# Values kept per head pair in DRAM, and transposes that take every second to fourth column

## The chip, the cores and the metric

The kernel runs on one core of a Trainium2 chip. The metric is the device time of one execution in microseconds; the time before is the median of three runs. Engines are named as the profile names them: PE (TensorE; PEld is its weight load), DVE (VectorE), ACT (ScalarE), POOL (GpSimd), SP (the engine that issues nearly all transfers).

## The reference, cut to what matters

An encoder layer over two sequences, a prompt of 256 tokens (a grid of 4 rows by 64 columns) and a sample of 2048 tokens (32 rows by 64 columns), model width 1024. A projection gives q, k, v and a gate for a neighbourhood attention with 8 heads of 64, and two more parts for a Fourier mixing branch. Both branches are normalised, gated, joined and projected back.

```python
proj = rms_norm(x, g_pre) @ w_in
q, k, v, z_a, u_f, z_f = split(proj)
# attention: a query at (r, c) sees the keys of 8 rows by 16 columns around it
logits = einsum(q, k_window) * scale + bias
p = softmax(logits)
y_a = einsum(p, v_window)
y_f = fft2(u_f).real @ w_f + b_f
out = x + rms_norm(concat(rms_norm(y_a)*silu(z_a), rms_norm(y_f)*silu(z_f)) @ w_out, g_post)
```

## The kernel before, in words

Everything is float32; the large products are made of three products of rounded parts each (`mm3`). The kernel first runs the input projection, stage by stage, and stores q, k, v, gates and the Fourier input in DRAM tensors (up to about 548 us of the profile). Then come the Fourier branch's transforms (to about 613 us), attention (to about 850 us), and the last output projection. The order of the work on every engine is written out by hand: `vu`, the loop over `i` and `j` of the projection with its hooks, and in attention one loop over `k` in which each engine's instructions are issued in a fixed order. SP works through one queue of transfers in program order and waits in it.

**v on its way to attention.** `put_rows` stores a finished tile of v of the sample (128 tokens by 512 features, all 8 heads) in the DRAM tensor `vN`, indexed by column half, row, column and feature (L361, 16 tiles of v and 16 of u, u into `uN`). Six copies from DRAM to DRAM (`v_copy`, L368, one per step `i` from 9 to 14 of the projection) gather from `vN` the four column blocks of 23, 31, 31 and 24 columns that attention reads, into `vD[0]` to `vD[3]`, each with 32 rows. The prompt's v is stored apart, in `vP`.

**Attention in groups.** There are 4 head pairs (128 features) and 9 groups for each: group 0 is the prompt, groups 1 to 8 are four row windows of the sample (11, 15, 15 or 12 key rows, `NR`, from row `K0`) times two column halves. Each group has two column blocks, so its keys number rows times columns, 160 to 465 for each block. `scores` makes the logits (L1225), `bias_max` and `exps` the exponentials, `soft` (L1259, POOL) divides by the sums; all stand in the tile `w`, 128 queries by keys, for two heads.

The product with v needs the keys on the partitions. So a block of n keys is cut into m pieces of at most 128 keys, with m from 2 to 4. `prep_v` loads the pieces of v, with z partitions (a multiple of 8) to a piece, and lists them in `g["ch"]` as (first column, number of keys, place in the tile `v`). `transp` (L1577) transposes each piece of `w` on PE into PSUM: the piece is loaded as weights, the identity of 128 columns streams through. ACT copies the first head's pieces to SBUF (L1579), DVE the second's (L1581). `pv` (L1593) multiplies each piece with its piece of v. Before the change, piece x is the consecutive keys from z*x on:

```python
z = min(-(-n // m) + 7 & ~7, 128)
ch = [(z * x, min(z, n - z * x), j + x) for x in range(m)]
```

For n = 465 that gives pieces of 120, 120, 120 and 105 keys. Over a head pair there are 55 pieces, each for two heads: 440 transposes and 880 products in the kernel. The load of v takes 512 B per key and partition, since one key's 128 features of the head pair stand in a row of 512 floats.

In the loop over `k`, the group k gets its scores while the group k - 1 is transposed and multiplied with v; the load of v for group k + 1 (`prep_v`) is issued at the end of step k. The tile `v` has three buffers (`VB`).

Of the kernel before, what the change touches and what calls it, by code (L numbers as in the profile page):

```python
# [10 lines left out]
F32 = mybir.dt.float32  # L11
# [19 lines left out]
K0 = (0, 4, 12, 20)  # L31
KW = (23, 31, 31, 24)
# [142 lines left out]
def build(tc, A, O):  # L175
    nc = tc.nc
# [3 lines left out]
    dr = es.enter_context(tc.tile_pool(name="dr", bufs=1, space=DRAM))  # L180
# [1 line left out]
    qD = dr.tile([4, 128, T], F32, name="qD")  # L182
    kD = dr.tile([4, 128, T], F32, name="kD")

    vD = [dr.tile([32, w, 512], F32, name="vD%d" % i) for i, w in enumerate(KW)]
    vP = dr.tile([2, 4, 40, 512], F32, name="vP")
    zD = dr.tile([2, 512, T], F32, name="zD")
    ZD = dr.tile([128, 16, 512], F32, name="ZD")
    uD = dr.tile([TP, 512], F32, name="uD")

    vN, uN = [dr.tile([2, 32, 32, 512], F32, name=n) for n in ("vN", "uN")]
    sD = dr.tile([5, 128, 4, 512], F32, name="sD")
    xD = dr.tile([7, 128, 4, 512], F32, name="xD")
    ivD = dr.tile([18, 128], F32, name="ivD")
# [5 lines left out]
    ident = cst.tile([128, 128], F32, name="ident")  # L200
# [24 lines left out]
    def mmt(n):  # L225
        x = mmc[0] % 5 > 2
        mmc[0] += 1
        return ps.tile([128, n], F32, tag="t" if x else "a", name="mm", bufs=2 if x else 3)
# [115 lines left out]
    def vu_out(m, c):  # L344
        s, b = PL[c]
        o = st.tile([128, 512], F32, tag="f", name=m + "o", bufs=3)
        x = row_tile(c)
        nc.scalar.activation(o, acc.pop((m, c)), AF.Copy, scale=invt[:, x:x + 1])
        if s is not None:
            put_rows(m, 0, b, s, o)  # L350
        elif m == "u":
            nc.sync.dma_start(uD[c * 128:c * 128 + 128, :], o)
        else:
            for r in range(4):
                nc.sync.dma_start(vP[c, r, 8 * c:8 * c + 32], o[32 * r:32 * r + 32])
                x = 24 * (1 - c)
                nc.sync.dma_start(vP[1 - c, r, 32 * c:32 * c + 8], o[32 * r + x:32 * r + x + 8])

    def put_rows(m, sg, b, s, o):
        r = 16 * sg + 4 * s  # L360
        nc.sync.dma_start((vN if m == "v" else uN)[b, r:r + 4].rearrange("r c e -> (r c) e"), o)  # L361


    VC = ((0, 0, 0, 23, 0), (1, 0, 8, 24, 0), (1, 1, 0, 7, 24), (2, 0, 24, 8, 0), (2, 1, 0, 23, 8), (3, 1, 8, 24, 0))

    def v_copy(i):
        x, b, c0, n, d0 = VC[i]
        nc.sync.dma_start(vD[x][:, d0:d0 + n], vN[b][:, c0:c0 + n])  # L368


    uu_ = {}
# [125 lines left out]
    def vu(sg, S, hooks):  # L497
# [7 lines left out]
        for i, (j, s) in enumerate(seq):  # L505
            for x in loads.get(i, ()):
                op_load(x)
            if i in splits:
                op_split(splits[i])
            for f in hooks.get(i, ()):  # L510
                f()
            p = mmt(512)
            h, l = op_[j]
            th, tl = bnew[sg, j]
            for k in range(4):
                mm3(nc, p, th[:, k, 128 * s:128 * s + 128], tl[:, k, 128 * s:128 * s + 128], h[k // 2][:, k % 2],
                    l[k // 2][:, k % 2], k == 0, k == 3)
            T2 = lambda o, a: nc.vector.tensor_tensor(out=o, in0=a, in1=p, op=ALU.add)
            if j == 0:
                uc[s] = et("uc")  # L520
                nc.scalar.copy(uc[s], p)
            elif j == 2:
                T2(uc[s], uc[s])
            elif j == 3:
                u4[s] = et("u4")
                T2(u4[s], uc[s])
            else:
                o = st.tile([128, 512], F32, tag="f", name="vuo", bufs=3)
                T2(o, (u4 if j in (4, 6) else uc)[s])
                if j == 4:  # L530
                    T2(uc[s], uc[s])
                put_rows("v" if j in (1, 6) else "u", sg, int(j in (4, 6)), s, o)
# [104 lines left out]
    for kp in range(4):  # L637
        ks = slice(2 * kp, 2 * kp + 2)
        v = part(RV[kp // 2], kp)
# [131 lines left out]
    for b in range(16):  # L771
# [13 lines left out]
        if 2 <= b < 8:  # L785
            x, y = divmod(b, 2)
# [9 lines left out]
        p = mmt(512)[:, :TP]  # L796
# [3 lines left out]
        o = st.tile([128, 256], F32, tag="f", name="f", bufs=3)  # L800
        if kind % 2:
            i, d = p, o
        else:
            i = p.rearrange("p (b r c) -> p b r c", b=2, c=32)
            d = o.rearrange("p (r b c) -> p b r c", b=2, c=32)
# [47 lines left out]
    for i in range(16):  # L853
        sg, pr = divmod(i, 8)
# [14 lines left out]
        o = [st.tile([128, 1024], F32, tag="f", name="f", bufs=3) for x in range(2)]  # L869
# [31 lines left out]
        for j in range(7):  # L901
            for f, d in ((u_load, 0), (u_split, 4), (u_stage1, 6)):
                x = 7 * pr + j - 7 - d
# [33 lines left out]
            if sg == 0:  # L937
                x, y = divmod(7 * (pr - 1) + j, 14)
# [27 lines left out]
            if 9 <= i < 15 and j == 2:  # L966
                v_copy(i - 9)
            p = mmt(512)
# [34 lines left out]
    ptb = [ps.tile([128, 512], F32, tag="t", name="ptb", bufs=2) for i in range(2)]  # L1003
# [179 lines left out]
    def prep_v(g):  # L1183
        cs = slice(g["pr"] * 128, g["pr"] * 128 + 128)
        g["v"] = jl.tile([128, 7, 128], F32, tag="v", name="v", bufs=VB)
        g["ch"], j = [], 0
        for b, (c0, w) in enumerate(g["t"]):
            n = g["nr"] * w
            src = (vP[b] if g["R"] is None else vD[2 * g["hc"] + b][K0[g["R"]]:]).rearrange("r c e -> (r c) e")
            m = -(-n // 128)  # L1190
            z = min(-(-n // m) + 7 & ~7, 128)
            f = m if src.shape[0] >= m * z else n // z
            nc.sync.dma_start(g["v"][:z, j:j + f], src[:z * f, cs].rearrange("(j p) e -> p j e", p=z))
            if f < m:
                nc.sync.dma_start(g["v"][:n - z * f, j + f], src[z * f:n, cs])
            ch = [(z * x, min(z, n - z * x), j + x) for x in range(m)]
            g["ch"].append(ch)
            j += len(ch)
        g["za"] = jl.tile([128, 256], F32, tag="za", name="za", bufs=VB)
        nc.sync.dma_start(g["za"], zD[1, cs, g["ts"]])  # L1200

# [69 lines left out]
    for g in G[:2]:  # L1271
        prep(g)
        prep_v(g)
# [11 lines left out]
    for t, (g, x) in enumerate(zip(G, (0, 640))):  # L1285
        g["w"] = []
        for c0, w in g["t"]:
            n = 2 * g["nr"] * w
# [281 lines left out]

    def transp(g, b):
        ch = g["ch"][b]
        n, z = len(ch) * 128, ch[0][1]
        o = jp.tile([128, 2, 512], F32, tag="pt", name="pt", bufs=PB)
        for h in range(2):
            for j, (c0, nk, v) in enumerate(ch):
                nc.tensor.transpose(ptb[h][:nk, j * 128:j * 128 + 128], g["w"][b][:, h, c0:c0 + nk], ident)  # L1577
            if h == 0:
                nc.scalar.copy(o[:z, h, :n], ptb[h][:z, :n])  # L1579
            else:  # L1580
                V.tensor_copy(o[:z, h, :n], ptb[h][:z, :n])  # L1581
        g["pt"] = g.get("pt", []) + [o]
# [109 lines left out]
    def part(P, name, n):  # L1692
        return [sm.tile([128, n, 128], F32R, tag="y%s%d" % (x, n) if n < 4 else "y" + x, name="y" + x,
                        bufs=3 if n == 4 else 1) for x in "hl"]
# [103 lines left out]
    prep(G[4])  # L1798
    f_mm(0)
    transp(G[0], 0)  # L1800
    f_norm(range(2))
    transp(G[0], 1)
    soft(G[1], 1)
    run_later()
# [4 lines left out]
    pv(G[0])  # L1809
    ys_load(ftiles[2])  # L1810
    prep_v(G[2])
    split_q(G[3])
    prep(G[5])
    ones32 = sm.tile([128, 32], F32, name="ones32", bufs=1)
    nc.vector.memset(ones32, 1.0)
    for k in range(2, len(G) + 1):
        pr, i = divmod(k, 9)
        g, f = G[k] if k < len(G) else None, G[k - 1] if k else None
# [14 lines left out]
        if k == 28:  # L1833
            for c, x in enumerate(("kh", "kl")):
                w = kp.tile([128, T], F32R, tag=x, name="wk")
                WO[c] = [w[:, 56 + D * y:56 + D * y + D] for y in range(2)]
        if k in WK:
            c, y = WK[k]
# [3 lines left out]
        x = k // 2 + 1  # L1842
# [11 lines left out]
        if not g:  # L1854
            a_mm(atiles[0], 0, range(6))
        transp(f, 0)
        if g:
            exps(g, 0, 1)
# [57 lines left out]
        if k + 1 < len(G):  # L1916
            prep_v(G[k + 1])
# [123 lines left out]
```

## Time and profile before

| | us |
|---|---|
| median of three runs | 959.93 (957.2 to 960.42) |
| profiled execution | 958.19 |
| its span, first to last instruction | 956.4 |
| PE busy | 944.8 (99% of the span) |
| PE weight loads busy | 784.3 (82%) |
| DVE / ACT / POOL busy | 732.0 / 505.8 / 453.3 |

The granted clock of PE is 0.997 over the span. The DMA queue that carries nearly everything moves 270.68 MB in 140,352 packets and takes 82.9% of the sixteen DMA engines' time. A line such as "L1577 PE MATMUL ptb<-ident,w 128*120 128x128 f32 x204 | 33.1, 278" names the source line, the engine, the operation, the output and inputs, the weights' rows and columns (128*120), what streams through (128x128), the count, and then the busy time in us and the mean duration of one in ns. Durations of matmuls overlap, so what one costs is read from the spacing of their starts.

### The profile page before, as it was taken

To read this page: it belongs to the slowest core of one execution; us is meant where nothing else is said; L and a number is where in the kernel's file an instruction comes from. 1 tells how busy PE (TensorE), PEld (TensorE's weight loads), DVE (VectorE), ACT (ScalarE), POOL (GpSimd) and SP (SyncE) were. 2 spreads that over 40 slices of the span, in tenths; PEclk is the share of its full clock that TensorE was granted. 3 is DMA by queue.
4 is the path that set the end of the run, shared out by engine and by line. 5 is a ranking of instruction groups with operands and counts; after the bars stand their busy time and mean duration, and the time that the engine had idled before them with its cause. 6 is when DMAs were issued, how large, how long until landed. Compare 5 with 4: busy or idle time off the path is not lost.

```text
span 956.4 us, 16730 instructions
## 1 busy us (share of the span) xinstructions
PE 944.8 (99%) x5595; PEld 784.3 (82%) x5595; DVE 732.0 (77%) x1347; ACT 505.8 (53%) x1088; POOL 453.3 (47%) x426
## 2 busy tenths in 40 slices
PE   9999999999999999999999999999999999999996
PEld 7889988888888888888888879788787888788885
DVE  6758987788876765698887369777888878759876
ACT  6835676433334532233344267677876777654443
POOL 4100002464751302575566045567899798624444
PEclk9999999999999999999999999999999999999998
DMA  9899697557848894499889996698998999889995
GB/s 356 298 385 336 243 339 270 189 201 270 299 188 323 314 341 144 175 352 361 300 289 338 338 341 246 215 276 281 309 253 253 290 280 312 239 296 327 305 317 197
DMA packets 140790, 272.17 MB, mean 285 GB/s; under 512 B 12854, under 2 KB 80664, under 8 KB 137440
## 3 DMA queue, kind: packets, MB, share of 16 engines
q1 hardware_dynamic: 140352, 270.68, 82.9%
q8 instruction: 45, 0.74, 0.3%
q10 hardware_dynamic: 288, 0.40, 0.1%
q14 instruction: 41, 0.34, 0.1%
q0 software_dynamic: 64, 0.02, 0.0%
HBM read 181.37 MB, written 96.81 MB: 291 GB/s over the span
## 4 chain that ended last, share of the span: by engine, by line
PE 89%; DMA 4%; DVE 2%; POOL 2%; ACT 1%; issue 1%; SPq 0%; DVEq 0%; POOLq 0%; ACTq 0%
PE mm L166 18%; PE mm L164 18%; PE mm L165 18%; PE po L1504 10%; PE ptb L1577 5%; PE pv L1593 5%; PE s L1225 4%; DMA yr<-yD 2%; PE px L1689 2%; PE pz L1689 2%; DMA yo<-xt 1%; PE py L164 1%; PE py L165 1%; PE py L166 1%; PE ptb L1043 1%
## 5 line engine op out<-in xcount | busy, mean ns | idle before, releaser
L164 PE MATMUL mm<-xh,wa 128*128 128x512 f32 x448 | 174.4, 389 | 0.0
L166 PE MATMUL mm<-xh,wa 128*128 128x512 f32 x448 | 174.3, 389 | 0.0
L165 PE MATMUL mm<-xl,wa 128*128 128x512 f32 x448 | 174.3, 389 | 0.0
L545 POOL TENSOR_TENSOR ws<-wr 128x512 f32<-128x512 f32 x16 | 22.6, 1415 | 219.3 <-DMA wr<-wz 215.6
L1259 POOL TENSOR_SCALAR w<-w,m 128x465 f32<-128x465 f32 (+9 forms) x136 | 89.3, 670 | 32.7 <-DVE m L1256 13.5
L165 PEld LDWEIGHTS mm<-xl,wa 128*128 128x128 f32 x448 | 84.1, 188 | 17.5
L164 PEld LDWEIGHTS mm<-xh,wa 128*128 128x128 f32 x448 | 84.1, 188 | 17.5
L166 PEld LDWEIGHTS mm<-xh,wa 128*128 128x128 f32 x448 | 84.1, 188 | 17.4
L560 DVE TENSOR_TENSOR wa<-wr,wa 128x512 fp32r<-128x512 f32 x60 | 75.4, 1264 | 21.9 <-ACT wa L559 21.6
L1504 PE MATMUL po<-wk,yh 128*128 128x512 f32 x280 | 87.1, 392 | 0.9 <-ACT yh L1490 0.9
L1252 ACT ACTIVATE w<-w,m 128x465 f32<-128x465 f32 (+9 forms) x136 | 78.4, 579 | 14.3 <-DVE m L1247 13.6
L1968 POOL TENSOR_TENSOR xt<-of,xt 128x512 f32<-128x512 f32 x34 | 43.2, 1293 | 54.6 <-issue 33.0
L1247 DVE CUSTOM_DVE_ANT_1 w<-s,tb 128x465 f32<-128x465 f32 (+8 forms) x124 | 61.4, 529 | 8.9 <-PE s L1225 8.0
L598 POOL TENSOR_TENSOR mt<-mt,rmask 128x880 f32<-128x880 f32 (+2 forms) x24 | 50.3, 2111 | 32.6 <-DVE mt L594 26.2
L164 PE MATMUL mm<-vh,xh 128*128 128x512 f32 x168 | 65.4, 389 | 0.0
L165 PE MATMUL mm<-vl,xh 128*128 128x512 f32 x168 | 65.4, 389 | 0.0
L166 PE MATMUL mm<-vh,xl 128*128 128x512 f32 x168 | 65.4, 389 | 0.0
L1504 PEld LDWEIGHTS po<-wk,yh 128*128 128x128 f32 x280 | 52.1, 188 | 12.2 <-ACT yh L1490 1.3
L891 DVE TENSOR_TENSOR f<-u,mm 128x512 f32<-128x512 f32 x64 | 43.4, 679 | 23.3 <-PE mm L166 18.5
L1577 PE MATMUL ptb<-ident,w 128*120 128x128 f32 (+8 forms) x422 | 59.0, 277 | 1.4 <-ACT pt L1579 1.2
L559 ACT CAST wa<-wr 128x512 fp32r<-128x512 f32 x60 | 36.5, 618 | 43.5 <-PE mm L166 20.4
L1577 PEld LDWEIGHTS ptb<-ident,w 128*120 128x120 f32 (+8 forms) x422 | 47.1, 140 | 14.5 <-issue 4.6
(332 smaller groups left out, 2469.3 us busy)
## 6 DMA issues: line engine op xcount, KB each, us to landing
wr<-wz SPq DMA_DIRECT2D x48, 512.0 KB
vl<-sD SPq DMA_DIRECT2D x20, 512.0 KB
xm<-xm SPq DMA_DIRECT2D x9, 1024.0 KB
oD<-ofs SPq DMA_DIRECT2D x18, 512.0 KB
of<-oD SPq DMA_DIRECT2D x18, 512.0 KB
xt<-xn SPq DMA_DIRECT2D x18, 512.0 KB
yo<-xt SPq DMA_DIRECT2D x35, 256.0 KB
yr<-yD SPq DMA_DIRECT2D x34, 256.0 KB
```

Source lines behind the costliest of these rows:

```text
L164: nc.tensor.matmul(out, lh, rh, start=first, stop=False)
L165: nc.tensor.matmul(out, lh, rl, start=False, stop=False)
L166: nc.tensor.matmul(out, ll, rh, start=False, stop=last)
L560: nc.vector.tensor_tensor(out=o[:, 1], in0=src, in1=o[:, 0].bitcast(F32), op=ALU.subtract)
L598: nc.gpsimd.tensor_tensor(out=o, in0=i, in1=rmask[:, m0:m0 + n].unsqueeze(2).to_broadcast([128, n, 80]), op=ALU.add)
L891: nc.vector.tensor_tensor(out=dst(f, b), in0=src(uu[u]), in1=src(p), op=op)
L1247: nc.vector.tensor_tensor_reduce(out=rows(g["w"][b][:, h, :n], w), in0=rows(g["s"][2 * b + h][:, :nr * sw(w)], sw(w))[:, :, :w], in1=tv, s ...
L1252: nc.scalar.activation(w, w, AF.Exp, bias=m[:, h:h + 1], scale=-1.0, accum_out=m[:, 2 + h:3 + h])
L1259: nc.gpsimd.tensor_scalar(w, w, m[:, 4 + h:5 + h], 1.0, ALU.mult, ALU.mult)
L1504: nc.tensor.matmul(p, (d["l"] if x == 2 else d["h"])[:, c], w(n, int(x == 1), c), start=j == 0, stop=j == 11)
L1577: nc.tensor.transpose(ptb[h][:nk, j * 128:j * 128 + 128], g["w"][b][:, h, c0:c0 + nk], ident)
L1593: nc.tensor.matmul(p[hs, b], g["v"][:nk, v, hs], g["pt"][b][:nk, h, j * 128:j * 128 + 128], start=j == 0, stop=j == len(ch) - 1)
```

## The change

v of the sample is stored per head pair: `vN` and `vD` get the head pair as an outer dimension and rows of 128 floats, so that consecutive keys of one head pair follow each other in memory. A store of v writes four pieces of 512 B for each partition. `prep_v` puts m consecutive keys on one partition, so one packet of the load has 2 to 4 keys; piece x of a block is now the keys x, x + m, x + 2m and so on. `transp` therefore takes every m-th column of `w`, and takes an even number of them where the tile is wide enough (one column more than needed, whose result is not used). The loads still cover a multiple of 8 partitions, where the tensor's end allows it, else a multiple of 16 and a second load for the rest. The number of keys in a piece becomes nearly equal: for n = 465, 118, 116, 116 and 116 columns are transposed.

```diff
-    vD = [dr.tile([32, w, 512], F32, name="vD%d" % i) for i, w in enumerate(KW)]
+    vD = [dr.tile([4, 32, w, 128], F32, name="vD%d" % i) for i, w in enumerate(KW)]
...
-    vN, uN = [dr.tile([2, 32, 32, 512], F32, name=n) for n in ("vN", "uN")]
+    vN = dr.tile([2, 4, 32, 32, 128], F32, name="vN")
+    uN = dr.tile([2, 32, 32, 512], F32, name="uN")
...
     def put_rows(m, sg, b, s, o):
         r = 16 * sg + 4 * s
-        nc.sync.dma_start((vN if m == "v" else uN)[b, r:r + 4].rearrange("r c e -> (r c) e"), o)
+        if m == "v":
+            nc.sync.dma_start(vN[b, :, r:r + 4].rearrange("h r c e -> (r c) h e"), o.rearrange("p (h e) -> p h e", h=4))
+        else:
+            nc.sync.dma_start(uN[b, r:r + 4].rearrange("r c e -> (r c) e"), o)
...
     def v_copy(i):
         x, b, c0, n, d0 = VC[i]
-        nc.sync.dma_start(vD[x][:, d0:d0 + n], vN[b][:, c0:c0 + n])
+        nc.sync.dma_start(vD[x][:, :, d0:d0 + n], vN[b][:, :, c0:c0 + n])
...
             n = g["nr"] * w
-            src = (vP[b] if g["R"] is None else vD[2 * g["hc"] + b][K0[g["R"]]:]).rearrange("r c e -> (r c) e")
             m = -(-n // 128)
-            z = min(-(-n // m) + 7 & ~7, 128)
-            f = m if src.shape[0] >= m * z else n // z
-            nc.sync.dma_start(g["v"][:z, j:j + f], src[:z * f, cs].rearrange("(j p) e -> p j e", p=z))
-            if f < m:
-                nc.sync.dma_start(g["v"][:n - z * f, j + f], src[z * f:n, cs])
-            ch = [(z * x, min(z, n - z * x), j + x) for x in range(m)]
-            g["ch"].append(ch)
-            j += len(ch)
+            z = -(-n // m) + 1 & ~1
+            if g["R"] is None:
+                src = vP[b].rearrange("r c e -> (r c) e")
+                nc.sync.dma_start(g["v"][:z, j:j + m], src[:, cs].rearrange("(p j) e -> p j e", j=m))
+            else:
+                src = vD[2 * g["hc"] + b][g["pr"]].rearrange("r c e -> (r c) e")
+                k0 = K0[g["R"]] * w
+                y = z + 7 & ~7
+                y = y if k0 + y * m <= src.shape[0] else z & ~15
+                for p0, p1 in ((0, y), (y, z)):
+                    if p0 < p1:
+                        nc.sync.dma_start(g["v"][p0:p1, j:j + m],
+                                          src[k0 + p0 * m:k0 + p1 * m].rearrange("(p j) e -> p j e", j=m))
+            g["ch"].append([(x, -(-(n - x) // m), j + x) for x in range(m)])
+            j += m
...
     def transp(g, b):
         ch = g["ch"][b]
-        n, z = len(ch) * 128, ch[0][1]
+        m, z = len(ch), ch[0][1] + 1 & ~1
+        n = 128 * m
...
             for j, (c0, nk, v) in enumerate(ch):
-                nc.tensor.transpose(ptb[h][:nk, j * 128:j * 128 + 128], g["w"][b][:, h, c0:c0 + nk], ident)
+                y = nk + 1 & ~1
+                y = y if c0 + m * y - m < g["w"][b].shape[2] else nk
+                nc.tensor.transpose(ptb[h][:y, j * 128:j * 128 + 128], g["w"][b][:, h, c0:c0 + m * y - m + 1:m], ident)
```

## The prediction

> **What bounds the kernel now.** I read the page's parts 1 and 2 first, then the time by stretches, then what TensorE waited for, then the groups of the lines that the diff touches.
>
> ```profile
> span 956.4 us, 16730 instructions
> PE 944.8 (99%) x5595; PEld 784.3 (82%) x5595; DVE 732.0 (77%) x1347; ACT 505.8 (53%) x1088; POOL 453.3 (47%) x426
> DMA  9899697557848894499889996698998999889995
> DMA packets 140790, 272.17 MB, mean 285 GB/s; under 512 B 12854, under 2 KB 80664, under 8 KB 137440
> PE 89%; DMA 4%; DVE 2%; POOL 2%; ACT 1%; issue 1%; SPq 0%; DVEq 0%; POOLq 0%; ACTq 0%
> ...
> 613.00:740.00 127.00, 125.80 (x1115) 100.84 (x1115) 100.71 (x301) 97.47 (x277) 103.00 (x124) 1.00 0.92 271
> 740.00:850.00 110.00, 109.66 (x993) 88.89 (x991) 84.77 (x252) 76.11 (x218) 80.84 (x112) 1.00 0.96 281
> 850.00:948.00 98.00, 97.14 (x444) 79.81 (x439) 78.35 (x174) 44.31 (x125) 42.23 (x34) 1.00 0.90 300
> 948.00:956.40 8.40, 0.42 (x4) 0.27 (x3) 5.18 (x14) 1.52 (x6) 2.99 (x3) 0.71 0.44 158
> ```
>
> The first number after a stretch's length is PE's busy time. Attention's transposes and products run from 613 to 850 us: PE lacks 127.00 - 125.80 = 1.20 us there and then 110.00 - 109.66 = 0.34 us; in the last projection it lacks 0.86 us. The DMA engines are busy too (0.92, 0.96), but a busy DMA engine only costs time where PE waits for it. So the next view is what PE waited for, the whole list:
>
> ```profile
> PE ptb L1577 <- ACT pt L1579: 1.2, 2, 0.7
> PE idle L237 <- POOL onesq L233: 1.0, 1, 1.0
> PE po L1504 <- ACT yh L1490: 0.9, 1, 0.9
> PE ptb L1577 <- POOL ysq L1614: 0.2, 1, 0.2
> PE mm L170 <- DVE xl L296: 0.2, 1, 0.2
> ```
>
> The columns are waiter and releaser, microseconds in total, times, longest wait. No DMA stands in it. The kernel is a queue of TensorE work; a change in it counts at full price, and a change elsewhere counts for at most the 2.4 us that PE lacks between 613 and 948 us (1.20 + 0.34 + 0.86).
>
> **The change part by part.**
>
> *1. The loads of v (the loop in prep_v).* 84 issues before (L1193 with 72, L1195 with 12), 84 after: one per window and column block, and a second one for the three narrow blocks of the last window row, in each of 4 head pairs. By the nine sizes of issue (from the view of DMA issues, the first and the last in the fence below) they move 12,456 KB, in rows of 128 floats (512 B): 24,900 packets. After, one packet holds 2, 3 or 4 keys; counting the partitions that the new code loads (1,992 per head pair) gives about 8,000. Writing v by head pair turns 16 stores of 128 packets into 16 of 512: +6,100. The six DRAM copies go from 32 runs to 128 each: +600. In all 140,790 becomes about 130,500, with the same bytes. The gain is hidden completely: each load is issued about two groups before its products, into three buffers, and no row of PE's waits names it. So I set it to 0, with 2.4 us as the most that it could give back.
>
> ```profile
> v<-vD SPq DMA_DIRECT2D x24, 180.0 KB
> ...
> v<-vD SPq DMA_DIRECT2D x4, 42.0 KB
> ...
> L1193 SPq DMA_DIRECT2D v<-vD x64: 311/452/2680, 562.5 to 830.4; - x64
> L361 SPq DMA_DIRECT2D vN<-vuo x12: 319/320/867, 128.4 to 385.8; - x12
> L368 SPq DMA_DIRECT2D vD<-vN x6: 473/474/564, 412.8 to 516.5; - x6
> SPq L361 <- DVE vuo L518: 60.7, 22, 7.8
> ```
>
> *2. The stores and copies.* The three numbers after an L line's count are the shortest, median and longest issue in ns. A store whose partitions each hold four pieces should issue like the loads of several pieces (452 ns) and no longer like one piece (320 ns): 16 x 0.13 = 2.1 us of SP's time. Queued behind it on SP are the stores of u, the weight loads and the reloads of u. SP's queue stood 60.7 us at this very line waiting for VectorE's results, so it has that time. DVE, ACT and POOL gain no instruction. Cost 0; if the cover went, 2.1 us spread over 350 us. The copies keep their 473 ns issues and their bytes; what they could cost otherwise is a rival below.
>
> *3. The copies out of PSUM, and the products with v.* The counts do not change: 440 transposes by the code (4 head pairs, 2 heads, 55 pieces), as many PSUM-to-SBUF copies over the same 256 to 512 columns, 880 products. A copy covers fewer partitions (114 to 124 in place of 120 or 128), a product contracts fewer rows, which costs the same at 128, 120 and 105 rows (283, 277 and 272 ns). Cost 0.
>
> ```profile
> L1593 PE MATMUL pv<-pt,v 120*64 120x128 f32 x416 | 30.7, 277 | 0.0
> L1593 PE MATMUL pv<-pt,v 105*64 105x128 f32 x96 | 9.5, 272 | 0.0
> L1593 PE MATMUL pv<-pt,v 128*64 128x128 f32 x80 | 6.9, 283 | 0.0
> ```
>
> *4. The transposes: where the price is open.* A transpose loads a piece of w as weights and streams the 128 columns of the identity. The piece was consecutive columns; now it is every 2nd (48 transposes), 3rd (264) or 4th (128) column, an even number of them, 80 to 128.
>
> ```profile
> L1577 PEld LDWEIGHTS ptb<-ident,w 128*120 128x120 f32 x204 | 23.3, 137 | 8.8 <-issue 3.8 <-POOL w L1259 1.8 <-POOL kl L1141 0.9
> L1577 PEld LDWEIGHTS ptb<-ident,w 128*105 128x105 f32 x48 | 8.2, 171 | 0.0
> L1577 PEld LDWEIGHTS ptb<-ident,w 128*128 128x128 f32 x38 | 4.8, 140 | 1.3
> L1577 PEld LDWEIGHTS ptb<-ident,w 128*80 128x80 f32 x24 | 2.5, 118 | 1.1 <-issue 0.4 <-POOL yr L1481 0.2
> ...
> 638.85 1.04 PE L1577 MATMUL ptb<-ident,w 128*120 128x128 f32 x8
> 639.64 0.48 PE L1504 MATMUL po<-wo,yh 128*128 128x512 f32 x1
> ...
> 646.80 0.82 PE L1577 MATMUL ptb<-ident,w 128*120 128x128 f32 x6
> 647.37 0.71 PE L1504 MATMUL po<-wo,yh 128*128 128x512 f32 x2
> ...
> L1551 PEld LDWEIGHTS ptb<-sqs,ones x32: 106/108/110, 619.3 to 657.9; 128*32 128x32 f32 x32
> L1034 PEld LDWEIGHTS pup<-f,up x4: 135/137/160, 567.4 to 567.7; 128*32 128x32 f32 x4
> L1034 PEld LDWEIGHTS ptb<-f,up x16: 186/192/192, 565.4 to 567.1; 128*128 128x128 f32 x16
> ```
>
> First the spacing. Six transposes of 120 columns start at 646.80, and the next product at 647.37; eight transposes, of which the program makes two of 105 columns, take 638.85 to 639.64. The two more cost 0.79 - 0.57 = 0.22 us, so 110 ns each, odd pieces or not. The identity's stream sets this; the load for the next transpose runs beside it and is free as long as it streams in under about 109 ns.
>
> Then the loads. Even pieces: 118 ns for 80 columns, 140 for 128, which is 22 / 48 = 0.46 ns per column over a fixed 81 ns. The odd piece: (171 - 81) / 105 = 0.86 ns per column, nearly twice that, and yet free, because 105 x 0.86 = 90 ns is under 109. So evening out the odd pieces gains 0.
>
> Now the step. The trace has one load with a step, the 32 columns that the code takes eight apart for up (pup): 137 ns against 108 ns for 32 consecutive ones. With the same 81 ns that is 1.75 against 0.84 ns per column, a factor of 2.1. It is an ordinary load; the changed transposes step by 2 to 4. Ends for the price: below, 0 (a load that is free cannot become freer); above, 1.75 ns per column for every stepped piece, so 203 ns in place of 109 at 116 columns. Summed over the 440 pieces by width (48 of 114, 144 of 116, 32 of 118, 48 of 120, 48 of 124, the rest narrower or 126 and 128) that end is +37.6 us. Between them: if the pairwise fetch of even pieces survives and only slows by the same factor, 2.1 x 0.46 = 0.96 ns per column; 116 columns then take 111 ns (2 over), 120 take 115 (6 over), 124 take 119 (10 over), in sum +1.5 us. I take half of that, +0.8 us: the row of odd pieces shows that a halved rate is hidden, and the steps are shorter than the eight that was measured. What is hidden here is hidden by the identity's stream; beyond 109 ns every ns is paid 440 times on the bounding engine.
>
> **Sum.** 0 + 0 + 0 + 0.8. The profiled execution took 958.19 us (span 956.4 and 1.8 around it); the median of the three runs, 959.93, is 1.7 above it. 958.2 + 0.8 = 959.0 us, between the two.
>
> **The rivals.**
>
> *Slower, the fetch goes by stretches of memory.* At 1.75 ns for a column that has its stretch to itself, and 0.46 ns where columns are adjacent, a stretch holds 1.75 / 0.46 = 3.8, so four columns. Then step 2 costs 0.88 ns per column (free up to 124 columns), step 3 has four columns on three stretches, 1.31 ns (152 ns at 116 columns), step 4 costs 1.75 (203 ns). Summed by width: 0.0 + 9.8 + 12.1 = +22 us, 980 us. It decides from about 0.94 ns per column on, where a piece of 116 passes 109 ns. For it: the 3.8 comes out near a whole number. Against: consecutive odd columns come at 0.86 ns, so the even rate is a second way of fetching, two at a time, and not the memory's limit; two ways side by side need not fall to the slowest.
>
> This rival is also a rule of the Trainium skill, page "SBUF — State Buffer", section "Door 1: The DMA port swizzle (why `[64,N]` ≈ `[32,N]`)": lines of 16 bytes, full rate only with at least two accesses on the same line. It speaks against this change, steps of 12 and 16 bytes leave one or two columns to a line; by that rule the sum would be 980 us, and the trace agrees with the rule as far as the stretch of 3.8 columns goes.
>
> *Slower, every step costs 1.75 ns per column:* +37.6 us, 996 us. For it: the only stepped row. Against: that step is 32 bytes, twice the largest here.
>
> *Slower, the copies of v go on few DMA engines.* Their outermost dimension becomes 4. If a copy were spread over four engines, 6.8 MB at the 285 GB/s of all sixteen (24 us) would occupy those four for 96 us between 412 and 516 us, where the weight loads also need them, and PE would starve for 20 to 50 us. Against: the two outer dimensions have one common stride on both sides and can be taken as 128 rows.
>
> *Faster:* the waits of PE between 613 and 948 us vanish with the smaller DMA load: at most -2.4 us, 955.8 from the profiled execution, 957.5 from the median. For it: DMA at 0.96. Against: PE's waits name ACT and POOL.
>
> **How the numbers follow.** What a measurement of this kernel can tell from no change is about 0.3%, 2.9 us. Forecast (price of the step 0 to 1.5 us): 0.62, range of its own 956 to 962.5. Stretches: 0.19. Full price: 0.08. Copies on few engines: 0.04. Faster by over 0.3%: 0.07, since even all waits gone is 2.4 us. So faster 0.07, same 0.62, slower 0.31. The range goes from 955.8 to 982: it takes in the stretches and leaves out the full price, the copies and a little below, some 0.14.
>
> **What would show it.** Right: the transposes' loads last longer (up to 190 ns) but eight of them still take 0.79 us; PE's busy share stays 99%; packets near 130,500; no DMA among PE's waits. Wrong: the loads of four-step pieces show 250 ns or more and a run of eight takes 1.1 us or longer (stretches give 7 x 0.20 us), PE's time in the two attention stretches then grows by 10 to 40 us; or PE waits between 412 and 548 us for weights (copies). A result below 956 would mean that DMA traffic slowed PE in a way that no row of waits shows.

## The result: 0.22% slower, and the profile after

| | before | changed |
|---|---|---|
| median of 17 runs, us | 959.06 | 961.17 |
| ratio to before | | 1.0022 (95% interval 1.0013 to 1.0032) |
| span of the profiled execution, us | 956.4 | 960.3 |
| DMA packets | 140,790 | 131,342 |

The change costs 0.0022 x 959.06 = 2.1 us. The page and the time by stretches of the changed kernel (columns as before):

```profile
span 960.3 us, 16733 instructions
...
PE 947.9 (99%) x5595; PEld 788.1 (82%) x5595; DVE 729.2 (76%) x1347; ACT 507.0 (53%) x1088; POOL 454.4 (47%) x426
...
DMA packets 131342, 272.17 MB, mean 283 GB/s; under 512 B 12910, under 2 KB 70768, under 8 KB 127672
...
413.00:548.00 135.00, 135.00 (x597) 111.67 (x595) 97.67 (x109) 48.95 (x83) 67.62 (x39) 1.00 0.94 332
...
613.00:740.00 127.00, 126.00 (x1101) 101.87 (x1097) 100.84 (x300) 97.33 (x276) 102.12 (x123) 1.00 0.88 270
740.00:850.00 110.00, 109.76 (x982) 90.29 (x982) 84.50 (x253) 76.44 (x219) 81.63 (x113) 1.00 0.91 277
```

The transfers did what the change says: 9,400 packets fewer, and in attention the DMA engines' share falls from 0.92 and 0.96 to 0.88 and 0.91. PE's idle time there hardly moves (1.00 and 0.24 us, from 1.20 and 0.34), yet the counts in the same two stretches fall from 1115 and 993 matmuls to 1101 and 982. PE counts as busy as before and gets through less.

How much less is read from the line of the transposes, before and after: the last two times in each row's head are the first and the last start.

```profile
L1577 PE MATMUL ptb<-ident,w x422: 270/273/329, 613.6 to 847.2; 128*120 128x128 f32 x68, 128*105 128x128 f32 x17, 128*96 128x128 f32 x14, 128*128 128x128 f32 x14
```

```profile
L1590 PE MATMUL ptb<-ident,w x422: 270/273/387, 613.8 to 849.0; 128*116 128x128 f32 x48, 128*120 128x128 f32 x16, 128*124 128x128 f32 x16, 128*114 128x128 f32 x14
```

From 613.6 to 847.2 is 233.6 us, from 613.8 to 849.0 is 235.2: +1.6 us. The median duration is the same 273 ns, but the longest went from 329 to 387 ns. One run of six transposes that follows the scores shows which one that is (timelines of PE and PEld, first the kernel before, then the changed one):

```profile
636.39 0.33 PE L1225 MATMUL s<-kh,ql 64*128 64x360 f32 x2
636.65 0.66 PEld L1577 LDWEIGHTS ptb<-ident,w 128*120 128x120 f32 x6 [0.23 <-issue]
636.65 0.87 PE L1577 MATMUL ptb<-ident,w 128*120 128x128 f32 x6
637.28 0.48 PE L1504 MATMUL po<-wo,yh 128*128 128x512 f32 x1
```

```profile
636.80 0.32 PE L1235 MATMUL s<-kh,ql 64*128 64x360 f32 x2
637.05 0.72 PEld L1590 LDWEIGHTS ptb<-ident,w 128*116 128x116 f32 x6 [0.23 <-issue]
637.05 0.92 PE L1590 MATMUL ptb<-ident,w 128*116 128x128 f32 x6
637.73 0.48 PE L1514 MATMUL po<-wo,yh 128*128 128x512 f32 x1
...
647.18 0.27 PE L1570 MATMUL pn<-ident,nsb 128*128 128x128 f32 x1
647.18 0.73 PEld L1590 LDWEIGHTS ptb<-ident,w 128*120 128x120 f32 x6
647.28 0.82 PE L1590 MATMUL ptb<-ident,w 128*120 128x128 f32 x6
647.86 0.48 PE L1514 MATMUL po<-wo,yh 128*128 128x512 f32 x1
```

After the scores, the run from its start to the next product's start took 0.63 us and now takes 0.68. A run of six that follows another full matmul takes 0.58 us (0.57 before). So a run in the middle of PE's work is as fast as it was, and one after the scores is 50 ns slower. In the starts of the instructions those 50 ns lie wholly between the first and the second transpose (161 ns before, 211 after); from then on the spacing is 109 ns in both. In the run of 637.05 the first weight load and the first matmul start within 3 ns of each other, after PEld had been idle for 0.23 us; in the run of 647.28 the first load starts 0.10 us ahead of its matmul, beside the product before. So after the scores' 64-row products the first load isn't started ahead and nothing covers it. Why it isn't started ahead is not shown: the profile names no wait there (issue). The load's duration is then paid, and the stepped load is longer:

```profile
L1590 PEld LDWEIGHTS ptb<-ident,w 128*116 128x116 f32 x144 | 18.9, 187 | 2.1 <-issue 1.4 <-POOL w L1269 0.2 <-POOL ysum L1727 0.2
L1590 PEld LDWEIGHTS ptb<-ident,w 128*124 128x124 f32 x48 | 6.3, 193 | 0.7
L1590 PEld LDWEIGHTS ptb<-ident,w 128*88 128x88 f32 x24 | 3.0, 157 | 0.5
```

88 columns take 157 ns, 124 take 193: (157 - 81) / 88 = 0.86 and (193 - 81) / 124 = 0.90 ns per column where consecutive even columns took 0.46. Without cover 116 columns then cost 0.88 x 116 = 102 ns, against 0.46 x 120 = 55: 47 ns per run. Of the 72 runs, 37 had such a long second spacing before (mean 158 ns) and 40 have it now (202 ns): (40 x 202 - 37 x 158) - 3 x 109 = 1.9 us. The long spacing goes with what runs ahead: 36 of the runs follow a product over 64 rows, and all 36 have the long spacing in both kernels (141 to 166 ns before, 178 to 223 after). The other four runs with it now are three behind an idle stretch of PE and one behind a product with a single column. Over all runs of transposes, from the start of the matmul ahead to the start of the second matmul behind, the sum went from 84.6 to 86.7 us, +2.1 us.

The other 2 us between the two profiled spans lie behind the last transpose. PE's wait for `yh` in the last projection, 1.9 us in place of 0.9, is one of the two:

```profile
PE po L1514 <- ACT yh L1500: 1.9, 2, 1.2
```

That part comes and goes from execution to execution: the second experiment has the same transposes and a span of 957.9.

### The profile page after: what moved, and what is told of

Read it like the earlier page. It is cut to its first block, busy times and chain, and to the rows that moved or that the text cites. A ratio compares the mean times of both kernels' runs of the same rounds, so it can differ in the third digit from the quotient of the medians.

```text
span 960.3 us, 16733 instructions
## 1 busy us (share of the span) xinstructions
PE 947.9 (99%) x5595; PEld 788.1 (82%) x5595; DVE 729.2 (76%) x1347; ACT 507.0 (53%) x1088; POOL 454.4 (47%) x426
## 2 busy tenths in 40 slices
DMA packets 131342, 272.17 MB, mean 283 GB/s; under 512 B 12910, under 2 KB 70768, under 8 KB 127672
## 4 chain that ended last, share of the span: by engine, by line
PE 92%; DVE 3%; DMA 2%; ACT 1%; issue 1%; POOL 1%; DVEq 0%; SPq 0%; POOLq 0%; ACTq 0%
PE mm L165 18%; PE mm L166 18%; PE mm L164 18%; PE po L1514 13%; PE ptb L1590 5%; PE pv L1606 5%; PE s L1235 4%; PE px L1702 2%; PE pz L1702 2%; DMA yr<-yD 1%; PE py L164 1%; PE py L165 1%; PE py L166 1%; PE ptb L1047 1%; ACT w L1262 1%
## 5 line engine op out<-in xcount | busy, mean ns | idle before, releaser
L564 DVE TENSOR_TENSOR wa<-wr,wa 128x512 fp32r<-128x512 f32 x60 | 70.9, 1190 | 20.2 <-ACT wa L563 20.0
L1590 PEld LDWEIGHTS ptb<-ident,w 128*116 128x116 f32 (+9 forms) x422 | 52.2, 182 | 13.1 <-issue 5.8
L1590 PE MATMUL ptb<-ident,w 128*116 128x128 f32 (+9 forms) x422 | 61.2, 282 | 1.1 <-ACT pt L1592 1.0
```

Of the source, the lines that this page charges most:

```text
L564: nc.vector.tensor_tensor(out=o[:, 1], in0=src, in1=o[:, 0].bitcast(F32), op=ALU.subtract)
L1590: nc.tensor.transpose(ptb[h][:y, j * 128:j * 128 + 128], g["w"][b][:, h, c0:c0 + m * y - m + 1:m], ident)
```

## The experiments

Theory A: the loss is the first stepped weight load of a run, where nothing covers it. Theory B: every stepped transpose costs a little. Theory C: the transfers (split stores, copies in more runs, SP's order) cost it. The first four kernels ran side by side.

**1. The new layout with pieces of consecutive keys.**

```diff
-            z = -(-n // m) + 1 & ~1
...
+            z = min(-(-n // m) + 7 & ~7, 128)
+            f = m if src.shape[0] >= m * z else n // z
+            nc.sync.dma_start(g["v"][:z, j:j + f], src[:z * f].rearrange("(j p) e -> p j e", p=z))
...
-                nc.tensor.transpose(ptb[h][:y, ...], g["w"][b][:, h, c0:c0 + m * y - m + 1:m], ident)
+                nc.tensor.transpose(ptb[h][:nk, ...], g["w"][b][:, h, c0:c0 + nk], ident)
```

> v per head pair in DRAM as changed (split stores, copies in 128 runs), but pieces of consecutive keys again, so one key per packet and no stepped transposes. Theory A (the loss is the first stepped weight load of a run of transposes, where nothing covers it): ratio to before 1.000, within 0.1%; second spacing of a run after the scores 161 ns as before. Theory B (each stepped transpose costs a little, evenly): 1.000 as well. Theory C (the loss comes from the transfers: split stores, copies, the order in SP's queue): 1.002. Packets: about 147,500.

Measured: 958.85 us, ratio 1.0001 (0.9989 to 1.0013), 147,510 packets.

```profile
L1584 PE MATMUL ptb<-ident,w x422: 270/273/329, 613.8 to 847.4; 128*120 128x128 f32 x68, 128*105 128x128 f32 x17, 128*96 128x128 f32 x14, 128*128 128x128 f32 x14
```

From first to last transpose 233.6 us, as before. The split stores and the finer copies cost nothing, although here the DMA engines had more packets than in any other kernel. Theory C is out.

**2. The steps alone.** The DRAM tensors as before the change, keys on the partitions and transposes as after it.

```diff
-    vD = [dr.tile([4, 32, w, 128], F32, name="vD%d" % i) for i, w in enumerate(KW)]
+    vD = [dr.tile([32, w, 512], F32, name="vD%d" % i) for i, w in enumerate(KW)]
...
-                src = vD[2 * g["hc"] + b][g["pr"]].rearrange("r c e -> (r c) e")
+                src = vD[2 * g["hc"] + b].rearrange("r c e -> (r c) e")[:, cs]
```

> The other half alone: v in DRAM as before (rows of 512 floats, 512 B per key), m keys on a partition and stepped transposes as changed. Theories A and B: 1.002, all of the loss; the runs of transposes after the scores have a second spacing near 210 ns. Theory C: 1.000.

Measured: 961.29 us, ratio 1.0027 (1.0013 to 1.0041), 140,846 packets.

```profile
L1586 PE MATMUL ptb<-ident,w x422: 270/273/387, 613.8 to 849.0; 128*116 128x128 f32 x48, 128*120 128x128 f32 x16, 128*124 128x128 f32 x16, 128*114 128x128 f32 x14
```

235.2 us from first to last, the longest 387 ns: all of the loss, with the packets of 512 B. The changed kernel's larger packets give back nothing that these intervals can show.

**3. The changed kernel with a plain first transpose in each run**, 72 of 440.

```diff
+                s = 1 if h == j == 0 else m
-                nc.tensor.transpose(ptb[h][:y, ...], g["w"][b][:, h, c0:c0 + m * y - m + 1:m], ident)
+                nc.tensor.transpose(ptb[h][:y, ...], g["w"][b][:, h, c0:c0 + s * y - s + 1:s], ident)
```

> The changed kernel, but the first transpose of each run (first head, first piece) takes consecutive columns in place of its every m-th: it leaves out the right keys of that piece. 72 of 440 transposes change. Theory A: 1.0002 to 1.0005, nearly all of the loss is gone and the second spacing after the scores is back at 161 ns. Theory B: 72 of 440 make a sixth of the loss, 1.0018 stays. Theory C: 1.002.

Measured: 958.91 us, ratio 0.9998 (0.9987 to 1.0010).

```profile
636.68 0.87 PE L1591 MATMUL ptb<-ident,w 128*116 128x128 f32 x6
637.30 0.48 PE L1514 MATMUL po<-wo,yh 128*128 128x512 f32 x1
...
L1591 PE MATMUL ptb<-ident,w x422: 270/273/329, 613.6 to 847.3; 128*116 128x128 f32 x48, 128*120 128x128 f32 x16, 128*124 128x128 f32 x16, 128*114 128x128 f32 x14
```

The run is back at 0.62 us, the stretch at 233.7, the longest at 329 ns, although every transpose behind the first is still stepped, five of six in the run shown. The interval leaves theory B's 1.0018 out.

**4. The kernel before with a stepped first transpose in each run.**

```diff
+                s = len(ch) if h == j == 0 else 1
+                s = s if c0 + s * nk - s < g["w"][b].shape[2] else 1
-                nc.tensor.transpose(ptb[h][:nk, ...], g["w"][b][:, h, c0:c0 + nk], ident)
+                nc.tensor.transpose(ptb[h][:nk, ...], g["w"][b][:, h, c0:c0 + s * nk - s + 1:s], ident)
```

> The kernel before, but the first transpose of each run takes every m-th column where the tile is wide enough: it leaves out the right keys of that piece, all else is as before. Theory A: 1.0016 to 1.002, nearly the whole loss from one transpose in six to eight, second spacing near 210 ns. Theory B: 1.0003. Theory C: 1.000.

Measured: 959.76 us, ratio 1.0014 (1.0001 to 1.0026).

```profile
636.81 0.92 PE L1579 MATMUL ptb<-ident,w 128*120 128x128 f32 x6
637.48 0.48 PE L1504 MATMUL po<-wo,yh 128*128 128x512 f32 x1
...
L1579 PE MATMUL ptb<-ident,w x422: 270/273/386, 613.5 to 848.5; 128*120 128x128 f32 x68, 128*105 128x128 f32 x17, 128*96 128x128 f32 x14, 128*128 128x128 f32 x14
```

The run takes 0.67 us and the stretch 235.0. The ratio lies just below theory A's 1.0016 to 1.002, and by the total alone its interval still touches B's 1.0003; by the trace, one transpose in each run brings 1.4 of the 1.6 us. The sums over all 72 runs say the same: 85.0 us in experiment 3 and 86.4 here, against 84.6 before and 86.7 changed. Together with experiment 3 theory A is shown from both sides.

**5. Odd pieces left odd.**

```diff
-        m, z = len(ch), ch[0][1] + 1 & ~1
+        m, z = len(ch), ch[0][1]
...
-                y = nk + 1 & ~1
-                y = y if c0 + m * y - m < g["w"][b].shape[2] else nk
-                nc.tensor.transpose(ptb[h][:y, ...], g["w"][b][:, h, c0:c0 + m * y - m + 1:m], ident)
+                nc.tensor.transpose(ptb[h][:nk, ...], g["w"][b][:, h, c0:c0 + m * nk - m + 1:m], ident)
```

> The changed kernel without the evening out: pieces of 113, 115, 117 and 127 columns stay odd (14 of the 55 pieces of a head pair, 112 of 440 transposes); nothing is left out. In the changed kernel's trace two odd stepped loads of 113 columns took 230 and 237 ns, 1.35 ns per column over 81. If odd stepped loads stream at that rate, 115 columns take 155 ns and pass the identity's 109 by 46: 112 x 46 = 5 us more than the changed kernel, ratio to before 1.007. If oddness does not matter under a step (one column at a time either way, 0.88): ratio 1.002, as the changed kernel.

Measured: 965.04 us, ratio 1.0056 (1.0040 to 1.0072).

```profile
L1588 PE MATMUL ptb<-ident,w x422: 270/273/481, 613.6 to 853.5; 128*116 128x128 f32 x32, 128*115 128x128 f32 x16, 128*120 128x128 f32 x16, 128*124 128x128 f32 x16
...
L1588 PEld LDWEIGHTS ptb<-ident,w 128*117 128x117 f32 x32 | 9.2, 289 | 2.8 <-issue 2.4
L1588 PEld LDWEIGHTS ptb<-ident,w 128*115 128x115 f32 x48 | 8.2, 243 | 1.9 <-issue 1.2 <-POOL w L1269 0.5 <-POOL ysum L1725 0.2
L1588 PEld LDWEIGHTS ptb<-ident,w 128*113 128x113 f32 x14 | 3.2, 231 | 0.0
L1588 PEld LDWEIGHTS ptb<-ident,w 128*127 128x127 f32 x6 | 1.2, 195 | 0.4
```

With step 3, 113 odd columns stream at (231 - 81) / 113 = 1.33 ns, 150 ns and over the identity's 109; with step 4, 117 at (289 - 81) / 117 = 1.78; with step 2, 127 odd columns stay at 0.90. The odd pieces of steps 3 and 4 are no longer hidden even in mid-run: the spacing behind one is about 155 and 210 ns there in place of 109. From first to last transpose it is now 239.9 us, 4.7 more than in the changed kernel. The ratio puts the loss at 0.34%, some 3.3 us, with intervals wide enough to take in 4.7 and the 5 that were expected. That the expected sum came close is in part luck: 13 of a head pair's 55 pieces are odd, not 14, those of step 2 cost nothing and those of step 4 about twice the 46 ns assumed. Evening the pieces out is what keeps the stepped transposes nearly free.

**6. Rates by step.**

```diff
+                s = m
+                if m == 4:
+                    c0, y, s = 0, 60 - 2 * j - h, 2 ** j
-                nc.tensor.transpose(ptb[h][:y, ...], g["w"][b][:, h, c0:c0 + m * y - m + 1:m], ident)
+                nc.tensor.transpose(ptb[h][:y, ...], g["w"][b][:, h, c0:c0 + s * y - s + 1:s], ident)
```

> A look at the load's rate by step: in blocks cut into four pieces, piece 0 takes step 1, piece 1 step 2, piece 2 step 4, piece 3 step 8, with 60, 58, 56 and 54 columns for the first head and 59, 57, 55 and 53 for the second; it leaves out the right keys of those blocks. Theory of one column at a time: steps 2 and 4 last 81 + 0.88 per column (132 and 130 ns), step 1 even 81 + 0.44 (107 ns), step 1 odd 132 ns; step 8 as the ordinary stepped load of the kernel before, 1.75 per column (175 ns). Theory of memory stretches of four columns: step 2 0.88, step 4 already 1.75 (179 ns), step 8 1.75. The time itself says nothing here.

Measured (60 and 59 columns have step 1, 58 and 57 step 2, 56 and 55 step 4, 54 and 53 step 8):

```profile
L1593 PEld LDWEIGHTS ptb<-ident,w 128*55 128x55 f32 x16 | 2.8, 177 | 0.0
L1593 PEld LDWEIGHTS ptb<-ident,w 128*53 128x53 f32 x16 | 2.8, 176 | 0.0
...
L1593 PEld LDWEIGHTS ptb<-ident,w 128*58 128x58 f32 x16 | 2.1, 133 | 0.6
L1593 PEld LDWEIGHTS ptb<-ident,w 128*59 128x59 f32 x16 | 2.1, 133 | 0.0
L1593 PEld LDWEIGHTS ptb<-ident,w 128*57 128x57 f32 x16 | 2.1, 133 | 0.0
L1593 PEld LDWEIGHTS ptb<-ident,w 128*56 128x56 f32 x16 | 2.1, 130 | 0.0
L1593 PEld LDWEIGHTS ptb<-ident,w 128*54 128x54 f32 x16 | 2.0, 124 | 0.0
L1593 PEld LDWEIGHTS ptb<-ident,w 128*60 128x60 f32 x16 | 1.7, 107 | 3.6 <-issue 2.4 <-POOL kl L1145 0.8
```

Less 81 ns, per column: even 0.43, 0.90, 0.88, 0.80 for steps 1, 2, 4, 8; odd 0.88, 0.91, 1.75, 1.79. Neither expectation holds for all. Even loads have nearly one rate for every step over 1, step 8 too, where the first theory expected 1.75; odd loads have the rates that the stretches of four columns give from step 2 on (step 3, from experiment 5, has 1.33 where the stretches give 1.31).

## Why the prediction was right or wrong

**Part 1, the loads of v: right.** 131,342 packets against about 130,500. The gain was set to 0, and experiment 2 against the changed kernel shows none that the intervals can tell: no row of PE's waits named these loads.

**Part 2, the stores and copies: right.** Experiment 1 prices them together at 1.0001. The stores of v issue in 371 ns (320 before, 452 assumed), the copies in 476, and PE was busy for all of the 135 us in which the copies run, so the rival of copies on few engines did not come about.

```profile
L363 SPq DMA_DIRECT2D vN<-vuo x12: 359/371/816, 128.4 to 385.8; - x12
L372 SPq DMA_DIRECT2D vD<-vN x6: 475/476/585, 412.7 to 516.7; - x6
```

**Part 3, copies out of PSUM and products: right.** Experiment 3 has the changed kernel's copies and products with all their piece sizes, and is at 0.9998: they add nothing that its interval can show.

**Part 4, the transposes: a price per column near the middle case, the wrong cover.** The step was put between 0.46 and 1.75 ns per column, with 0.96 as the middle case; it is 0.88. That the middle case came near is in part luck: its reason was that the even rate slows by the factor of 2.1 measured at step 8, but even loads have nearly the same rate at steps 2, 4 and 8. That the step is hidden in mid-run held: eight transposes in a run that follows a full matmul take 0.80 us, from 0.79. The sentence that failed is "What is hidden here is hidden by the identity's stream". It was derived from two runs in mid-work and applied to all 440 transposes; but after the scores' 64-row products the first load has no such stream to run beside, and there it is paid, 47 to 50 ns more in some 40 runs. The term of +0.8 us stood for wide pieces that pass 109 ns in mid-run, and these cost about 0.2 us; the first loads, put at nothing, cost 1.9, and the two together are the 2.1. The trace of before had it on show: runs after the scores took 0.63 us for six transposes where the prediction's run took 0.57, and that difference lies in the second spacing, 161 against 109 ns.

**The sum.** 959.0 us was placed between the profiled execution and a median of three runs; the 17 runs of before then had a median of 959.06, so the point said "no change"; the ratio's interval lies wholly above 1, so the direction was missed, and the measured 961.17 is 2.2 us over the point. The forecast of a change within 0.3% and the range of 955.8 to 982 hold. That 0.3% is what a measurement can tell was too coarse: the interval of 17 runs is 0.1% to either side.

**The rivals.** Stretches of memory (980 us): the rates of odd loads agree with it from step 2 on, and so does the one ordinary load at step 8; but the change evens the pieces out, and the even loads came at about 0.88 at steps 2, 3 and 4 alike. The Trainium skill (page "SBUF — State Buffer", section "Door 1: The DMA port swizzle (why `[64,N]` ≈ `[32,N]`)") has the rule that lines of 16 bytes want two accesses each for full rate. The trace agrees with it for odd loads, full rate at step 2 (0.91) and half at step 4 (1.75), and not for even ones, whose rate is the same at step 2 as at step 4. Full price for every step (996 us): no even piece shows it. Faster by the waits: PE still lacks 1.00 and 0.24 us in attention.

## What to carry to other kernels

Where an operation is "hidden" by its neighbour, ask which ones have no such neighbour: here the first of a run, after 64-row products or an idle stretch of PE, pays in full, and their number times the difference is the price. Compare runs of the same instructions behind different predecessors before calling a cost zero. And on a kernel that PE fills to 99%, 9,400 packets fewer bought nothing, since no wait of PE named a transfer.

## What the runs showed of the hardware

By the fit of 118 ns at 80 columns and 140 ns at 128, a weight load of a float32 transpose takes 81 ns and then, for an even number of columns, 0.43 to 0.46 ns per consecutive column and about 0.88 (0.80 at step 8) at steps 2, 3, 4 and 8. With the same 81 ns an odd number takes 0.88 consecutive, 0.91 at step 2, 1.33 at step 3, 1.75 at step 4 and 1.79 at step 8. One column more can shorten the load: 56 columns at step 4 took 130 ns, 55 took 177. What of the engine makes the difference between even and odd stays open; only its rates were measured.

In mid-run transposes start 109 ns apart whatever their width from 53 to 120 columns, unless the load takes longer than that (111 ns apart at 124 stepped columns, 118 at 128). In all 36 runs behind a product over 64 rows the second transpose came later, by 32 to 57 ns with consecutive columns and by 69 to 114 with stepped ones. That this goes with the rows of the product ahead is shown by these runs; the reason is not.
